# One decoder layer in split fp32 on one core: the embedding projection moves to the head of the program, and the last gate's K units are made and taken in another order

## The chip, the cores and the metric

The program runs on one core of a Trainium2 chip. The metric is the device time of one execution in microseconds (us); lower is better. The kernel before took 2470.43 us, the median of three runs (2469.58 to 2470.85).

## What is computed

One layer on `x` (512 tokens, width 2048), all in float32. Three additions to `x` follow each other, and the last one is the one that the change is about:

```python
x = x + jnp.concatenate([a_out, r_out], axis=-1) @ w_o[i]      # attention and retention heads

h2 = rms_norm(x, g_ffn[i])
x = x + (jax.nn.silu(h2 @ w_gate[i]) * (h2 @ w_up[i])) @ w_down[i]   # DFF = 5632

gate = jax.nn.sigmoid(rms_norm(x, g_ple[i]) @ w_ple_gate[i] + b_ple_gate[i])
x = x + (p[i] @ w_ple_proj[i]) * gate                           # p: 512 x 256, w_ple_proj: 256 x 2048
```

`p @ w_ple_proj`, here called **the projection**, depends on the inputs alone. The gate needs the finished `x` of the feed-forward part: its K dimension is the 2048 columns of that `x`.

## The kernel before, in words

**Precision.** Every float32 operand is split in two float32r parts, high and low (`split`, line 55): ScalarE (ACT) copies the high part, VectorE (DVE) subtracts it from the source for the low part. A product then takes three matmuls (`mm3`, line 78): high by high (line 79), high by low (line 80) and low by high (line 81). A weight unit is 128x1024 values, 512 KB: one load on the SP queue, one copy `wh` on ACT, one subtraction `wl` on DVE.

**The first part** (to line 446) makes attention and retention. `rows` (line 86) takes four PSUM banks from a pool that holds four (`acc_p`, line 51), multiplies, and hands each bank to an `evac`. At the head the 16 chunks of `x` come in, each multiplied by its gain and split (`gained`, line 132) and squared for the norm (`squares`, line 139), while the first product `qk_attn` runs over eight weight units. Here a list scheduler sets the order on each engine.

**The second part** multiplies with a scheme of seven products for each 2x2 block of quarters. `ORDER` (line 458) names them 1, 5, 6, 3, 7, 2, 4. Each product p has factors of the activation (`factors`, line 477: sums and differences of quarters, each split, 7 ACT copies, 7 DVE subtractions and 4 DVE sums for a pair of K chunks) and a weight that is the sum of quarters: for 5, 6, 7 and 4 DVE adds one loaded quarter into another in place (`Group.add`, line 533). Then come `extract` (line 546: `wh` on ACT, `wl` on DVE, three buffers) and `multiply` (line 556: 12 matmuls). A **step** is one product of one K unit. The loop at line 817 runs over the steps: at step i it adds for step i+3, extracts for step i+2 and multiplies step i. A finished product is evacuated two steps later (`evacuate`, line 604, `later(2, go)`). Quarters of the output are ready after products 3, 7, 2 and 4.

**Groups.** Eleven groups make gate and up (four units each), six make `w_down` (`down(kg, n)`, line 723: K in three parts, output in two halves n), two make the last gate (`gate(n)`, line 783: four units, output in two halves). The K units of the last gate are the columns of `x`: units 0 and 1 come from half n = 0 of the last down product and go through DRAM (`spill` into `s_h3`, then `reload`). Unit 3 (nh = 1) is complete after product 7 of `down(2, 1)`, unit 2 (nh = 0) after its product 4. Their factors (`to_factors`, line 667: eight PE transposes `tp<-ident`, then `factors`) are made 6 and 8 steps after product 7's evacuation for unit 3, and 1 and 3 steps after product 4's for unit 2. `split_order` (line 704) makes the first gate group run products 1, 5, 6 for units (0, 1), then for units (2, 3).

**The projection** stands between the last down group and the first gate group: four `Plain` steps (line 574), each with one unit of `w_pp`, 24 matmuls into `tp` banks, four copies by ACT (line 601, `pp<-tp`) and four stores to DRAM (`ppd`). `load_p` (line 768) loads `pT` and splits it when product 7 of the group before begins. The gate's `finish` (line 791) reads the projection back.

Of the kernel before, what the change touches and what calls it, by code (L numbers as in the profile page):

```python
# [10 lines left out]
F32 = mybir.dt.float32  # L11
F32R = mybir.dt.float32r
# [5 lines left out]
P = 128  # L18
T = 512
# [14 lines left out]
def layer_kernel(ctx, tc, xT, pT, g_mix, wqk, wv, wg, qk_norm, g_ret, w_o, g_ffn,  # L34
# [17 lines left out]
    at_p = mix_ctx.enter_context(tc.tile_pool(name="at_p", bufs=2, space=PSUM))  # L52

# [357 lines left out]

    qk, v = qk_attn(0, load_rest), v_of(0)
# [42 lines left out]
    dram = ctx.enter_context(tc.tile_pool(name="dram", bufs=1, space=bass.MemoryType.DRAM))  # L455
# [49 lines left out]
    def later(n, fn):  # L505
        due.setdefault(now[0] + n, []).append(fn)

    class Group:
        def __init__(self, src, units, tiles, evac, order=None, after=lambda p: None):
            self.src, self.units, self.tiles, self.evac, self.after = src, units, tiles, evac, after  # L510
            self.raw, self.bank, self.w, self.next, self.plains = {}, {}, {}, None, None
            self.left = {p: len(units) for p in ORDER}
            steps.extend((self, p, u) for p, u in
                         (order or [(p, u) for p in ORDER for u in range(len(units))]))
# [7 lines left out]
        def load_next(self, q, u):  # L522
            n = len(self.units)
            if q == "11" and self.plains:
                for v in [u] + (list(range(u + 1, NS)) if u == n - 1 else []):
                    self.plains[v].load()
            elif self.next is not None:
                m = len(self.next.units)
                for v in [u] + (list(range(n, m)) if u == n - 1 else []):
                    if v < m:  # L530
                        self.next.load(q, v)
# [42 lines left out]
    class Plain:  # L574

        def __init__(self, n):
            self.n, self.then = n, None
            steps.append((self, "p", 0))

        def load(self):  # L580
            self.raw = raw_ab.tile([P, 2, T], F32, name="raw", tag="l1")
            nc.sync.dma_start(self.raw, w_pp[self.n])

        def add(self, p, u):
            pass

        def extract(self, p, u):
            self.wh = wq.tile([P, 2, T], F32R, name="wh", tag="wh")
            self.wl = wq.tile([P, 2, T], F32R, name="wl", tag="wl")
            split(self.wh, self.wl, self.raw)  # L590
            self.then()

        def multiply(self, p, u):
            for b in range(NB):
                o = tp_p.tile([P, T], F32, name="tp", tag="tp")
                at = slice(b * P, (b + 1) * P)
                for c in range(2):
                    mm3(o, pTH[c][0][:, at], pTH[c][1][:, at], self.wh[:, c, :], self.wl[:, c, :],
                        c == 0, c == 1)
                t = ev_tile("g", 4, name="pp")  # L600
                nc.scalar.activation(t, o, AF.Copy)
                nc.sync.dma_start(ppd[b][:, self.n], t)

    def evacuate(finish, ahead=None):

        def evac(g, p):
# [30 lines left out]
            later(2, go)  # L637
# [6 lines left out]
    s_h3 = {p: dram.tile([P, 4, 2, 256], F32R, name=f"h3_{p}") for p in ORDER}  # L644
    xd = [[dram.tile([P, NS, T], F32, name=f"x{i}_{b}") for b in range(NB)] for i in range(4)]
    ppd = [dram.tile([P, NS, T], F32, name=f"pp_{b}") for b in range(NB)]
# [57 lines left out]
    split_order = [(p, u) for us in ((0, 1), (2, 3)) for p in "156" for u in us] + \  # L704
                  [(p, u) for p in "3724" for u in range(4)]

    def reload(tiles, where, n, wait={}):
        def go(p):
            tiles[p] = sp.tile([P, 8, 2, 256], F32R, name="s" + p, tag="s" + p)
            nc.sync.dma_start(tiles[p][:, :n].bitcast(F32), where[p].bitcast(F32))  # L710
        return lambda p: later(wait[p], lambda: go(p)) if p in wait else go(p)
# [11 lines left out]
    def down(kg, n):  # L723
# [7 lines left out]
        def finish(th, nh, b, part, t):  # L731
# [12 lines left out]
            for u in range(2):  # L744
                k = 4 * n + 2 * nh + u
                sink = spill(s_h3, k) if n == 0 else into(s_e, k)
                later((1 if n == 0 or nh == 0 else 6) + 2 * u, lambda u=u, sink=sink: to_factors(
                    lambda b: outs[b, nh], 2 * u, sink, lambda c: gp[:, 4 * s + c:4 * s + c + 1]))
# [16 lines left out]
    pTH = []  # L765
    bias_t = []

    def load_p():
        for k in range(2):
            raw = ev_tile("A")  # L770
            nc.sync.dma_start(raw, pT[k * P:(k + 1) * P, :])
            pTH.append([late_pools["ev2"].tile([P, T], F32R, name="pT", tag="o", bufs=4) for _ in range(2)])
            split(*pTH[k], raw)
# [6 lines left out]

    plains = [Plain(n) for n in range(NS)]
# [25 lines left out]
    groups[-3].plains = plains  # L807
    for n, pl in enumerate(plains):
        pl.then = lambda n=n: groups[-2].load("11", n)
# [4 lines left out]
    p_at = steps.index((groups[-3], "7", 0))  # L814
    b_at = steps.index((groups[-2], "3", 0))
    i = -3
    while i < len(steps) or due:
        now[0] = i
        if i == p_at:
            load_p()  # L820
        if i == b_at:
            load_bias()
        for n, act in ((3, "add"), (2, "extract"), (0, "multiply")):
            if 0 <= i + n < len(steps):
                g, p, u = steps[i + n]
                getattr(g, act)(p, u)
# [75 lines left out]
```

## Time and profile before

| | |
|---|---|
| median of three runs | 2470.43 us (2469.58 to 2470.85) |
| the profiled execution's own time | 2470.09 us |
| its span (first to last instruction) | 2468.3 us |
| TensorE (PE) busy | 2385.4 us, 97%, 11434 matmuls |
| DVE busy | 1836.6 us, 74% |
| ACT busy | 1091.5 us, 44% |
| moved by DMA | 390.27 MB |

How to read it: a matmul counts as busy for about 0.39 us though the next one begins 0.227 us after it, so PE's busy share says little on how full it is; its waits and the granted clock (PEclk, 1.00 is 2.4 GHz, 0.50 is 1.2 GHz) say more. The same holds on a smaller scale for DVE and ACT: two equal instructions in a row take less than twice the time of one.

### The profile page before, as it was taken

To read this page: it belongs to the slowest core of one execution; us is meant where nothing else is said; L and a number is where in the kernel's file an instruction comes from. 1 tells how busy PE (TensorE), PEld (TensorE's weight loads), DVE (VectorE), ACT (ScalarE), POOL (GpSimd) and SP (SyncE) were. 2 spreads that over 40 slices of the span, in tenths; PEclk is the share of its full clock that TensorE was granted. 3 is DMA by queue.
4 is the path that set the end of the run, shared out by engine and by line. 5 is a ranking of instruction groups with operands and counts; after the bars stand their busy time and mean duration, and the time that the engine had idled before them with its cause. 6 is when DMAs were issued, how large, how long until landed. Compare 5 with 4: busy or idle time off the path is not lost.

```text
span 2468.3 us, 30337 instructions
## 1 busy us (share of the span) xinstructions
PE 2385.4 (97%) x11434; PEld 1994.3 (81%) x11434; DVE 1836.6 (74%) x2469; ACT 1091.5 (44%) x1628; POOL 70.3 (3%) x63
## 2 busy tenths in 40 slices
PE   9999999999999986999999999999999999996998
PEld 7888888888888865888888888888878788884777
DVE  7585664546363688888988889888888778894897
ACT  5333333423232355545555455545544344463643
POOL 1122020000000000000000000000000000000000
PEclk9999999999999988999999999999999999998999
DMA  5222332333333333356434554445766956768263
GB/s 192 86 79 76 94 94 85 112 99 103 100 105 100 100 122 98 125 171 195 143 129 136 183 180 144 124 148 189 301 239 222 376 175 219 269 240 341 100 212 120
DMA packets 127988, 390.27 MB, mean 158 GB/s; under 512 B 14944, under 2 KB 15328, under 8 KB 124256
## 3 DMA queue, kind: packets, MB, share of 16 engines
q1 hardware_dynamic: 125136, 384.12, 46.5%
q10 hardware_dynamic: 2704, 4.20, 0.7%
q8 instruction: 90, 1.47, 0.3%
q14 instruction: 58, 0.48, 0.1%
HBM read 311.19 MB, written 72.88 MB: 156 GB/s over the span
## 4 chain that ended last, share of the span: by engine, by line
PE 85%; DVE 6%; DMA 5%; ACT 2%; issue 1%; ACTq 0%; SPq 0%; DVEq 0%
PE acc L80 10%; PE acc L81 10%; PE acc L79 10%; PE Y L80 7%; PE Y L79 7%; PE Y L81 7%; PE Z L80 5%; PE Z L81 5%; PE Z L79 5%; PE X L81 5%; PE X L80 5%; PE X L79 5%; DVE wl L59 2%; DVE raw L468 2%; PE at L80 1%
## 5 line engine op out<-in xcount | busy, mean ns | idle before, releaser
L58 ACT ACTIVATE wh<-raw 128x1024 fp32r<-128x1024 f32 (+1 forms) x667 | 705.9, 1059 | 946.3 <-PE Y L81 225.2
L59 DVE TENSOR_TENSOR wl<-raw,wh 128x1024 fp32r<-128x1024 f32 (+1 forms) x667 | 811.8, 1222 | 367.5 <-ACT wh L58 365.3
L468 DVE TENSOR_TENSOR raw<-raw 128x1024 f32<-128x1024 f32 x296 | 358.1, 1222 | 28.6 <-DMA raw<-in_w_gu 14.7
L80 PE MATMUL Y<-wl,s 128*128 128x512 f32 x888 | 349.6, 394 | 0.3 <-DVE wl L59 0.3
L81 PE MATMUL Y<-wh,s 128*128 128x512 f32 x888 | 346.9, 391 | 0.0
L79 PE MATMUL Y<-wh,s 128*128 128x512 f32 x888 | 311.6, 392 | 18.9 <-ACT wh L58 18.9
L80 PE MATMUL acc<-wl,actH 128*128 128x256 f32 (+1 forms) x768 | 244.1, 320 | 1.5 <-DVE wl L59 1.3
L81 PE MATMUL acc<-wh,actL 128*128 128x256 f32 (+1 forms) x768 | 243.6, 320 | 0.0
L79 PE MATMUL acc<-wh,actH 128*128 128x256 f32 (+1 forms) x768 | 239.7, 320 | 1.7 <-ACT wh L58 1.7
L80 PE MATMUL X<-wl,s 128*128 128x512 f32 x592 | 233.4, 395 | 5.9 <-DVE wl L59 5.7
L80 PE MATMUL Z<-wl,s 128*128 128x512 f32 x592 | 234.3, 396 | 3.5 <-DVE wl L59 3.4
L81 PE MATMUL X<-wh,s 128*128 128x512 f32 x592 | 232.1, 393 | 1.8 <-DVE s L59 1.8
L81 PE MATMUL Z<-wh,s 128*128 128x512 f32 x592 | 230.8, 391 | 0.0
L79 PE MATMUL X<-wh,s 128*128 128x512 f32 x592 | 210.1, 394 | 5.3 <-ACT wh L58 5.0
L79 PEld LDWEIGHTS Y<-wh,s 128*128 128x128 f32 x888 | 167.2, 189 | 55.2 <-ACT wh L58 20.4
L79 PE MATMUL Z<-wh,s 128*128 128x512 f32 x592 | 208.7, 393 | 0.9 <-ACT wh L58 0.9
L80 PEld LDWEIGHTS Y<-wl,s 128*128 128x128 f32 x888 | 167.4, 189 | 35.5 <-DVE wl L59 1.4
L81 PEld LDWEIGHTS Y<-wh,s 128*128 128x128 f32 x888 | 167.4, 189 | 34.0
L80 PEld LDWEIGHTS acc<-wl,actH 128*128 128x128 f32 x768 | 146.1, 190 | 12.6 <-DVE wl L59 2.5
L79 PEld LDWEIGHTS acc<-wh,actH 128*128 128x128 f32 x768 | 144.5, 190 | 12.6 <-ACT wh L58 2.8
L81 PEld LDWEIGHTS acc<-wh,actL 128*128 128x128 f32 x768 | 145.7, 190 | 9.9
L79 PE MATMUL acc<-actH,wh 128*128 128x512 f32 x384 | 149.9, 390 | 0.0
(184 smaller groups left out, 3370.2 us busy)
## 6 DMA issues: line engine op xcount, KB each, us to landing
raw<-in_w_gu SPq DMA_DIRECT2D x176, 512.0 KB, 4.3
raw<-in_w_dn SPq DMA_DIRECT2D x88, 512.0 KB, 5.8
a<-o SPq DMA_DIRECT2D x154, 256.0 KB, 2.9
raw<-in_wqk SPq DMA_DIRECT2D x63, 512.0 KB, 3.5
s<-a SPq DMA_DIRECT2D x14, 2048.0 KB, 11.1
raw<-in_wv SPq DMA_DIRECT2D x32, 512.0 KB, 3.5
raw<-in_w_o SPq DMA_DIRECT2D x32, 512.0 KB, 3.6
xin<-x SPq DMA_DIRECT2D x64, 256.0 KB, 5.5
```

The lines of the kernel that those rows point to most:

```text
L58: nc.scalar.activation(H, src, AF.Copy)
L59: nc.vector.tensor_tensor(L, src, H.bitcast(F32), op=ALU.subtract)
L79: nc.tensor.matmul(o, aH, bH, start=start, stop=False, skip_group_check=goes_on)
L80: nc.tensor.matmul(o, aH, bL, start=False, stop=False, skip_group_check=goes_on)
L81: nc.tensor.matmul(o, aL, bH, start=False, stop=stop, skip_group_check=goes_on)
L468: nc.vector.tensor_tensor(o, x, y, op=ALU.add)
```

## The change

Four things change.

- The projection's code leaves the step list (`Plain`, `load_p` and the `plains` hooks go). It stands now before the first `qk_attn`, written with `rows`: two chunks of `pT` loaded and split, then four times one unit of `w_pp`, 24 matmuls into the four `acc` banks, four ACT copies `pp<-acc` (line 423 of the changed kernel) and four stores.
- Unit 3's factors are made 1 and 2 steps after product 7's evacuation, inside the last group's products 2 and 4. Its factor for product 4, whose SBUF tile is still in use, goes through DRAM (`s_h3["4"]` grows from 4 to 6 chunks). Unit 2's follow 1 and 2 steps after product 4's evacuation.
- `split_order` becomes units (0, 1), then (3), then (2). It is shared by the first gate-up group.
- To allow runs of one unit, `extract` of step i+2 now comes before `add` of step i+3, and product 5 is evacuated one step after its end, not two.

```diff
+    ppd = [dram.tile([P, NS, T], F32, name=f"pp_{b}") for b in range(NB)]
+    pTH = []
+    for k in range(2):
+        raw = rp_tile("raw")
+        nc.sync.dma_start(raw, pT[k * P:(k + 1) * P, :])
+        pTH.append(qk_pair())
+        split(*pTH[k], raw)
+    for n in range(NS):
+        def pp_evac(b, acc, n=n):
+            t = rp_tile("pp")
+            nc.scalar.activation(t, acc, AF.Copy)
+            nc.sync.dma_start(ppd[b][:, n], t)
+        rows([w_pp[n]], lambda k: pTH[k], pp_evac)
+
     qk, v = qk_attn(0, load_rest), v_of(0)
...
-    class Plain:
...
-            later(2, go)
+            later(1 if p == "5" else 2, go)
...
-    s_h3 = {p: dram.tile([P, 4, 2, 256], F32R, name=f"h3_{p}") for p in ORDER}
+    s_h3 = {p: dram.tile([P, 6 if p == "4" else 4, 2, 256], F32R, name=f"h3_{p}") for p in ORDER}
...
-    split_order = [(p, u) for us in ((0, 1), (2, 3)) for p in "156" for u in us] + \
+    split_order = [(p, u) for us in ((0, 1), (3,), (2,)) for p in "156" for u in us] + \
                   [(p, u) for p in "3724" for u in range(4)]
...
-                sink = spill(s_h3, k) if n == 0 else into(s_e, k)
-                later((1 if n == 0 or nh == 0 else 6) + 2 * u, lambda u=u, sink=sink: to_factors(
+                sink = spill(s_h3, k)
+                if n == 1:
+                    direct = into(s_e, k)
+                    sink = (lambda p, a=spill(s_h3, k - 2 * nh), b=direct: a(p) if p == "4" else b(p)) if nh else direct
+                later((1 + 2 * u) if n == 0 else (1 + u), lambda u=u, sink=sink: to_factors(
...
-        for n, act in ((3, "add"), (2, "extract"), (0, "multiply")):
+        for n, act in ((2, "extract"), (3, "add"), (0, "multiply")):
```

What this makes of the order on the engines is shown at three places.

**ACT at the head.** `wh` and `qkH` are copies for a split, `actH` a chunk of `x` with its gain, `sq` and `total` its square, `pp` a bank of the projection. Before, the first rows with work are these:

```order
L141 ACTIVATE total<-x_98 128x512
L61 ACTIVATE actH<-x_98,gm 128x512
L58 ACTIVATE wh<-raw 128x512
L61 ACTIVATE actH<-x_99,gm 128x512
L143 ACTIVATE sq<-x_99 128x512
L58 ACTIVATE wh<-raw 128x512
L58 ACTIVATE wh<-raw 128x1024
```

Now the list begins with the splits of `pT` and of two units of `w_pp`. Then come all 16 chunks of `x`, with the squares of eleven of them, four copies for the projection's first unit and the splits of the third and fourth `w_pp` unit among them. Only after these 33 rows stand the copies that empty the second unit's banks, here the first `pp` row:

```order
L62 ACTIVATE actH<-x_114,gm 128x512
L144 ACTIVATE sq<-x_110 128x512
L62 ACTIVATE actH<-x_115,gm 128x512
L423 ACTIVATE pp<-acc 128x512 x2
L144 ACTIVATE sq<-x_111 128x512
L423 ACTIVATE pp<-acc 128x512 x2
L144 ACTIVATE sq<-x_112 128x512
L59 ACTIVATE wh<-raw 128x512 x2
L144 ACTIVATE sq<-x_113 128x512
L144 ACTIVATE sq<-x_114 128x512
L423 ACTIVATE pp<-acc 128x512
L144 ACTIVATE sq<-x_115 128x512
```

The last `pp` row of this list belongs to the third unit; three more of it, with the norm's `sqs` among them, follow, and the fourth unit's four come after the next `wh`.

**PE where the last down group ends.** `Y_18616` and `Y_18837` are banks of its product 4, `tp<-wh,pT` is the projection, `X` a bank of the gate's product 1. Before:

```order
L80 MATMUL Y_18616<-wl,s_17545 128x512
L81 MATMUL Y_18616<-wh,s_17545 128x512
L79 MATMUL tp<-wh,pT 128x512
L80 MATMUL tp<-wl,pT 128x512
L79 MATMUL tp<-wh,pT 128x512
```

Now, with transposes `tp<-ident` of unit 3 in product 4 itself:

```order
L653 MATMUL tp<-ident,v 128x128 x2
L653 MATMUL tp<-ident,e_18533 128x128
L653 MATMUL tp<-ident,e_18534 128x128
L81 MATMUL Y_18836<-wl,s_17741 128x512
...
L81 MATMUL Y_18837<-wl,s_17741 128x512
L82 MATMUL Y_18837<-wh,s_17741 128x512
L81 MATMUL X_18942<-wl,s_18529 128x512
```

The gate's matmuls follow the last down matmul directly.

**DVE in the gate's single-unit steps.** `raw<-raw` adds weight quarters, `wl` is the subtraction of a weight, `s<-` and `t<-` are parts of `factors`. The last steps before product 3 read now:

```order
L482 TENSOR_TENSOR raw<-raw 128x1024
L479 TENSOR_TENSOR t_19072<-A,t_19071 128x256
L60 TENSOR_TENSOR wl<-raw,wh 128x1024
L60 TENSOR_TENSOR s_18531<-t_19071,s_18531 128x256
L479 TENSOR_TENSOR t_19074<-A,t_19072 128x256
L479 TENSOR_TENSOR t_19073<-A,t_19072 128x256
L60 TENSOR_TENSOR s_18569<-t_19072,s_18569 128x256
L482 TENSOR_TENSOR raw<-raw 128x1024
L60 TENSOR_TENSOR s_18636<-t_19074,s_18636 128x256
L60 TENSOR_TENSOR s_18702<-t_19073,s_18702 128x256
L60 TENSOR_TENSOR wl<-raw,wh 128x1024 x3
```

One weight is added to, split, added to again and split again, and the factors of unit 2 stand between. Between the head and the last down group the orders differ in a few rows near the first gate-up group's start (its unit 3 now before its unit 2); DVE's next 835 instructions stand as before.

## Rows read from the trace of the kernel before

**Rows 1.** The first section of the page: busy time of each engine, its share of the span, and instructions.
```profile
PE 2385.4 (97%) x11434; PEld 1994.3 (81%) x11434; DVE 1836.6 (74%) x2469; ACT 1091.5 (44%) x1628; POOL 70.3 (3%) x63
```

**Rows 2.** Busy time of each engine in stretches from the last down group into the first gate group; columns: stretch, its length, busy time of PE, its weight loads, DVE, ACT and POOL with their instructions, granted clock, DMA share, GB/s.
```profile
2205.00:2222.00 17.00, 17.00 (x79) 14.08 (x78) 16.67 (x26) 10.36 (x16) 0.00 (x0) 1.00 0.91 308
2222.00:2241.00 19.00, 18.93 (x84) 15.35 (x82) 16.62 (x26) 8.89 (x13) 0.00 (x0) 1.00 0.98 352
2241.00:2284.00 43.00, 19.06 (x58) 13.44 (x58) 8.57 (x12) 15.18 (x29) 0.00 (x0) 0.72 0.86 337
2284.00:2324.00 40.00, 36.55 (x167) 29.29 (x167) 36.08 (x62) 27.89 (x54) 1.01 (x1) 0.99 0.30 106
...
2254.00:2265.00 11.00, 4.01 (x9) 2.73 (x10) 0.69 (x1) 1.71 (x3) 0.00 (x0) 0.53 1.02 415
```

**Rows 3.** What PE waited for between 2165 and 2300 us: total, times, longest.
```profile
PE tp L79 <- ACT pT L58: 16.9, 2, 10.0
PE tp L79 <- ACT pp L601: 6.5, 2, 6.3
```

**Rows 4.** PE's matmuls in order of time: start, duration, line, operation, tiles, and in brackets the wait before it. The last down matmuls, the projection's first and some later ones, the gate's first matmul, and the first two of its product 3.
```profile
2240.32 0.39 PE L80 MATMUL Y<-wl,s 128*128 128x512 f32 x1
2240.54 0.39 PE L81 MATMUL Y<-wh,s 128*128 128x512 f32 x1
2247.83 0.80 PE L79 MATMUL tp<-wh,pT 128*128 128x512 f32 x1 [6.90 <-ACT pT L58]
2248.85 0.63 PE L79 MATMUL tp<-wh,pT 128*128 128x512 f32 x1
2249.28 0.63 PE L80 MATMUL tp<-wl,pT 128*128 128x512 f32 x1
...
2260.73 0.80 PE L79 MATMUL tp<-wh,pT 128*128 128x512 f32 x1 [9.97 <-ACT pT L58]
...
2283.45 0.73 PE L79 MATMUL X<-wh,s 128*128 128x512 f32 x2 [0.29 <-ACT wh L58]
...
2336.10 0.61 PE L79 MATMUL Z<-wh,s 128*128 128x512 f32 x2
```

**Rows 5.** The SP queue: when the two loads of `pT` were issued.
```profile
2227.67 0.33 SPq L771 DMA_DIRECT2D A<-in_pT  x1
...
2248.74 0.39 SPq L771 DMA_DIRECT2D A<-in_pT  x1
```

**Rows 6.** ACT in order of time: the split of the second `pT` chunk, and one of the projection's copies.
```profile
2260.05 0.63 ACT L58 ACTIVATE pT<-A 128x512 fp32r<-128x512 f32 x1 [6.41 <-DMA A<-in_pT]
...
2276.74 0.60 ACT L601 ACTIVATE pp<-tp 128x512 f32<-128x512 f32 x1 [2.44 <-PE tp L81]
```

**Rows 7.** DVE in order of time in the last down group: instructions of each size, pairs in one row (x2), and the instruction from which the sum below counts (the second evacuation of product 6).
```profile
2204.42 2.36 DVE L59 TENSOR_TENSOR wl<-raw,wh 128x1024 fp32r<-128x1024 f32 x2
...
2209.76 0.69 DVE L465 TENSOR_TENSOR v<-Y,e 128x512 f32<-128x512 f32 x1
2210.36 1.22 DVE L59 TENSOR_TENSOR wl<-raw,wh 128x1024 fp32r<-128x1024 f32 x1
2211.50 0.76 DVE L465 TENSOR_TENSOR t<-A,t 128x256 f32<-128x256 f32 x2
...
2226.02 1.28 DVE L465 TENSOR_TENSOR e<-Y,e 128x512 f32<-128x512 f32 x2
```

**Rows 8.** ACT in order of time at the head, and the first 30 us as in rows 2.
```profile
9.18 0.71 ACT L61 ACTIVATE actH<-x,gm 128x512 fp32r<-128x512 f32 x1
9.79 0.62 ACT L143 ACTIVATE sq<-x 128x512 f32<-128x512 f32 x1
10.31 0.71 ACT L61 ACTIVATE actH<-x,gm 128x512 fp32r<-128x512 f32 x1
...
17.21 1.04 ACT L58 ACTIVATE wh<-raw 128x1024 fp32r<-128x1024 f32 x1
18.15 0.71 ACT L61 ACTIVATE actH<-x,gm 128x512 fp32r<-128x512 f32 x1
...
0.00:30.00 30.00, 25.98 (x103) 18.55 (x104) 23.85 (x37) 24.34 (x39) 0.20 (x4) 1.00 0.81 274
```

**Rows 9.** PE in order of time at the head: its first real matmul, and its two waits.
```profile
5.35 1.20 PE L79 MATMUL acc<-wh,actH 128*128 128x512 f32 x4
...
18.30 1.19 PE L79 MATMUL acc<-wh,actH 128*128 128x512 f32 x4 [1.65 <-ACT wh L58]
20.64 0.50 PE L80 MATMUL acc<-wl,actH 128*128 128x512 f32 x1 [1.15 <-DVE wl L59]
```

**Rows 10.** The chain that ended last, at its beginning: start, duration, what. The load is the fifth; 1536 KB had been asked for with it.
```profile
2.59 5.60 DMA raw<-in_wqk
8.21 1.06 ACT wh L58
```

**Rows 11.** PE where the first gate-up group begins, in order of time, and the stretch around it as in rows 2.
```profile
947.53 1.22 PE L79 MATMUL Y<-wh,s 128*128 128x512 f32 x2 [16.34 <-ACT wh L58]
...
952.44 0.63 PE L80 MATMUL Y<-wl,s 128*128 128x512 f32 x1
952.86 0.63 PE L81 MATMUL Y<-wh,s 128*128 128x512 f32 x1
...
930.00:958.00 28.00, 8.94 (x27) 6.35 (x26) 25.06 (x52) 18.36 (x40) 0.00 (x0) 0.57 0.33 113
```

More of the change, by code (lines that the diff above doesn't have):

```diff
@@ L52, in layer_kernel @@
     at_p = mix_ctx.enter_context(tc.tile_pool(name="at_p", bufs=2, space=PSUM))
+    dram = ctx.enter_context(tc.tile_pool(name="dram", bufs=1, space=bass.MemoryType.DRAM))
     def split(H, L, src, scale=None):
@@ L454, in layer_kernel @@
     chain = ctx.enter_context(pool("chain", 1, space=PSUM))
-    dram = ctx.enter_context(tc.tile_pool(name="dram", bufs=1, space=bass.MemoryType.DRAM))
     late_pools = {}
@@ L510, in __init__ @@
             self.src, self.units, self.tiles, self.evac, self.after = src, units, tiles, evac, after
-            self.raw, self.bank, self.w, self.next, self.plains = {}, {}, {}, None, None
+            self.raw, self.bank, self.w, self.next = {}, {}, {}, None
             self.left = {p: len(units) for p in ORDER}
@@ L523, in load_next @@
             n = len(self.units)
[L524 to L527, printed above, removed]
+            if self.next is not None:
                 m = len(self.next.units)
@@ L572, in multiply @@
                 self.evac(self, p)
-    class Plain:
[L576 to L602, printed above, removed]
     def evacuate(finish, ahead=None):
@@ L643, in layer_kernel @@
     s_a = [{p: dram.tile([P, n, 2, 256], F32R, name=f"a{i}_{p}") for p in ORDER} for i, n in enumerate(KG)]
-    s_h3 = {p: dram.tile([P, 4, 2, 256], F32R, name=f"h3_{p}") for p in ORDER}
+    s_h3 = {p: dram.tile([P, 6 if p == "4" else 4, 2, 256], F32R, name=f"h3_{p}") for p in ORDER}
     xd = [[dram.tile([P, NS, T], F32, name=f"x{i}_{b}") for b in range(NB)] for i in range(4)]
-    ppd = [dram.tile([P, NS, T], F32, name=f"pp_{b}") for b in range(NB)]
     for i in range(NC // 2):
@@ L709, in go @@
             tiles[p] = sp.tile([P, 8, 2, 256], F32R, name="s" + p, tag="s" + p)
-            nc.sync.dma_start(tiles[p][:, :n].bitcast(F32), where[p].bitcast(F32))
+            nc.sync.dma_start(tiles[p][:, :n].bitcast(F32), where[p][:, :n].bitcast(F32))
+            if where is s_h3 and p == "4":
+                nc.sync.dma_start(tiles[p][:, 6:].bitcast(F32), where[p][:, 4:].bitcast(F32))
         return lambda p: later(wait[p], lambda: go(p)) if p in wait else go(p)
@@ L762, in layer_kernel @@
                                 s_d[kg], down(kg, n), None, after))
-    pTH = []
     bias_t = []
[L768 to L773, printed above, removed]
     def load_bias():
@@ L779, in load_bias @@
             bias_t.append(t)
-    plains = [Plain(n) for n in range(NS)]
     def gate(n):
@@ L806, in layer_kernel @@
         a.next = b
-    groups[-3].plains = plains
-    for n, pl in enumerate(plains):
-        pl.then = lambda n=n: groups[-2].load("11", n)
     for q in ("11", "12", "22"):
@@ L813, in layer_kernel @@
             groups[0].load(q, u)
-    p_at = steps.index((groups[-3], "7", 0))
     b_at = steps.index((groups[-2], "3", 0))
@@ L818, in layer_kernel @@
         now[0] = i
-        if i == p_at:
-            load_p()
         if i == b_at:
             load_bias()
-        for n, act in ((3, "add"), (2, "extract"), (0, "multiply")):
+        for n, act in ((2, "extract"), (3, "add"), (0, "multiply")):
             if 0 <= i + n < len(steps):
```

## The prediction

> **What bounds the kernel now.** I read the page's busy times first: PE is the busiest engine by far [rows 1], so a change pays where PE stands still. Next the waits of PE by stretch, and there one place stands out: between the last down group and the gate, PE waits 16.9 us for the splits of `pT` and 6.5 us for the projection's copies [rows 3]. The table by stretch shows what that place costs: from 2241 to 2284 PE issues 58 matmuls at a mean granted clock of 0.72, while the stretches before it run at 1.00 with PE full [rows 2]. At full speed a 512-column matmul follows the one before it after 0.227 us (2240.32, 2240.54 and on); inside the projection they stand 0.43 apart (2248.85, 2249.28), which is the lower level of 1.2 GHz, after a pause of 6.90 us [rows 4]. 50 matmuls at 0.227 and 8 short transposes of some 0.11 are 12.2 us of work in 43: **about 31 us are lost there.** The cause stands on the queue: the second `pT` load is issued 21 us after the first [rows 5], ACT waits 6.41 us for it [rows 6], and the DMA engines are then full (share 1.02 at 415 GB/s) [rows 2]. So the projection, meant to fill the time in which the gate's factors are made, waits itself.
>
> **What goes.** I measure the late stage from a point that both orders share, DVE's second evacuation of product 6 in the last down group, at 2209.76 [rows 7], to the first matmul of the gate's product 3, at 2336.10 [rows 4]: **126.3 us** before.
>
> **What stands there now.** The projection's 96 matmuls (21.8 us at 0.227) are gone from it, with their loads, splits, copies and stores. The rest is not PE's time alone, since all four `to_factors` calls of units 3 and 2 now fall into the steps of products 2 and 4 and the gate's first twelve. Counted in the new order, DVE has 117 instructions between the two points: 36 of 1024 elements, 62 of 256, 17 of 512 and two tiny ones. Two of 1024 in a row take 2.36 where one takes 1.22, so each takes 1.14; in the same way two of 256 take 0.76 and two of 512 1.28, one 0.69, which makes 0.34 and 0.60 [rows 7]. That is 41.0 + 21.1 + 10.2 + 0.3 = **72.6 us**. PE's own work in it, some 280 matmuls and 32 transposes, is 67 us, so DVE becomes the bound of this stage. After DVE's last subtraction PE still has the 12 matmuls of that step, 2.7 us. To this I add what DVE waits for. In the single-unit steps of products 5 and 6 a weight is added to, copied by ACT (1.04 us [rows 8]) and subtracted, one after the other, four times in all: 4.2 us if nothing fills them. And at its fullest DVE was busy for 16.67 of 17.00 us [rows 2], which is 1.4 us of small gaps here. The bounds are 75.3 (no wait at all) and 84 (all waits, and the last 12 matmuls at the lower clock, 2.4 more). I take 72.6 + 2.7 + 4.2 + 1.4, or **81**, since the order shows little between an addition and its subtraction. The late stage goes from 126.3 to 81, that is **-45.3 us**.
>
> **What is added at the head.** With no limit but PE the projection would take its 21.8 us there and a later start. The order on ACT is the limit. The four first loads are 1536 KB together; before, the load that completed as many bytes landed at 8.19 [rows 10], so ACT's second `wh` runs from 8.2 to 9.2. From there ACT has, in its order, 16 gained chunks at 0.61, 11 squares at 0.52, two `wh` at 0.94 [rows 8] and four copies at 0.50 (one lasts 0.60 [rows 6], a square 0.62 and 0.52 apart) before it may empty the second unit's banks: 19.4 us, to 28.6. The third unit needs these four banks, since the pool has four. The four copies and one square take to 31.1, then a square, two half splits and two squares to 33.7; the third unit's copies are done at 34.2, 35.2, 35.7 and, behind the norm's split, 36.8. The fourth unit's 24 matmuls run after these, to about 40.5. So `qk_attn` begins at **40.5 where it began at 5.35** [rows 9], 35.2 later. It then finds all of `x` split, and the two early waits of 1.65 and 1.15 [rows 9] should not return: **+32.4 us**, of which 21.8 is the projection and 10.6 is PE standing. Lower bound: ACT doesn't hold PE up, 21.8 less the two waits, +19. Upper: the third and fourth unit's 48 matmuls run at the lower clock and none of it is hidden, 0.2 each, +42.
>
> **What costs nothing.** The `w_pp` loads and stores share SP's queue with `x`; the first `wqk` load stands behind the stores of the first unit, whose last copy runs near 20 us, and must land by 40, so 20 us of the projection cover it. If the head were quick, the load would be late by some 5 us. Product 5's earlier evacuation needs two copies and one `wh` on ACT within one step, 1.0 + 0.95 of 2.72 us: nothing, or a microsecond in each of two groups. The swap of `extract` and `add` leaves DVE's order in the long middle as it was. In the first gate-up group unit 3 now comes before unit 2; the wait of 16.34 us there [rows 11] is before product 6 of the first units and stays. Its slow matmuls after it, 0.42 apart (952.44, 952.86), can come a few more or fewer: 0, within 3 us either way. Unit 3's factors for product 4 go out in two stores of 256 KB and come back with a reload that is read some twenty steps later.
>
> **The sum.** 2470.1 (the profiled execution's own time, 0.3 below the median of the runs) + 32.4 - 45.3 + 0 = **2457 us**.
>
> **Rivals.**
>
> *The head is lighter.* If the evacuations reach ACT earlier than I reckon, since ACT's instructions are partly shorter than I took them, the head costs +24 to +28 and the time is 2449 to 2453. For it: PE alone needs only 21.8. Against: the copies stand behind 33 rows on an engine that was busy for 24.34 of the first 30 us without the projection [rows 8].
>
> *The late stage stays long.* Either transfers bind again, or unit 2 is late all the same. The four rates from 2205 to 2324 times their lengths are 31 MB [rows 2], of which 7 go (`pT`, `w_pp` and 16 stores of 256 KB); 24 MB at 352 GB/s are 68 us and fit into 81, at 258, the mean over that time, they are 93. Or unit 2's chain of evacuation, transposes, copies and splits overruns the nine steps, 24 us at 12 matmuls each, that cover it. The stage then takes 90 to 93, and the time is 2466 to 2469: no change that can be told.
>
> *The clock at the head, slower.* PE now pauses between the second and third unit, from about 19 to 29 us. In the trace a pause of 9.97 us is followed by matmuls at the lower level, and after one of 16.34 us they were still 0.42 apart 5 us later [rows 4, 11]. The Trainium skill ("TensorE: Matmul & The Clock Gate", section "HAM oscillation — how this bites in real kernels") says that a matmul stream broken by waits falls back to half rate and starts cold after each of them, and by that rule moving the projection into a place with pauses gives part of the gain back. The trace agrees as far as the late stage goes (0.53 in 2254 to 2265 [rows 2]); no run here shows the head. By the rows the price is 0.2 us a matmul. In my forecast the 48 of the third and fourth unit wait for ACT anyway, so a slow start costs 0 to 5 us. The change would be slower if the lower level held through the fourth unit and the first three `qk_attn` units, 24 + 72 matmuls at 0.2, or 19 us: 2476. It decides from about 13 us, some 65 matmuls. Against it: PE is dense from 34 us on, and from 2284, PE busy again, the clock was at 0.99 [rows 2].
>
> *The change doesn't do what it says:* unit 3's factors could still wait for the tiles of the running group. The order shows their transposes inside product 4, so I give this little, within the second rival.
>
> **Chances.** Forecast, within 6 us of 2457: 0.60. Lighter head: 0.16. Late stage long: 0.17. Slow clock or other trouble at the head: 0.07. A measurement of this kernel can tell about 0.2%, 5 us, from no change. Faster by more: the first two and a little of the third, 0.79; the same: 0.15; slower: 0.06. The range runs from the lighter head to the late stage at its longest, **2447 to 2468**; what lies outside is the slow clock and a stage that gains nothing.
>
> **What would show each step.** Right: `qk_attn` begins at 38 to 43 us, with a PE wait of 7 to 11 us for an ACT `wh` or a bank near 20 to 29 us; no `pT` wait after 2200; DVE over 95% busy in the 70 us before the gate's product 3, which begins 77 to 84 us after the shared point. Wrong: a head under 30 us (evacuations earlier), PE idle with DVE idle too in the late stage (transfers, or unit 2's chain), or PEclk under 0.9 well past 45 us.

## The result and the profile after

The changed kernel took **2455.11 us** (median of four runs, 2454.82 to 2460.03) beside 2470.01 for the kernel before (four runs, 2468.43 to 2470.85): a ratio of 0.9945, interval 0.9928 to 0.9962. Five more runs later gave 2458.18 (2455.01 to 2462.65) and a ratio of 0.9944, interval 0.993 to 0.9957. The profiled execution took 2455.12 us with a span of 2453.3, against 2470.09 and 2468.3. The forecast of 2457.0 and its range hold.

The 15.0 us between the two profiled executions divide as follows. Up to the late stage each figure is how much more, or less, a matmul's start has shifted at the stretch's end than at its beginning, matmuls being counted from `qk_attn`'s first, without the two of the norm (`tp<-sqs`), which changed their place; the late stage has its own measure, below.

| stretch | forecast | measured |
|---|---|---|
| head, to 64 us of before | +32.4 | +32.9 |
| rest of the first part | 0 | -1.3 |
| start of the feed-forward part | 0, within 3 | -3.4 |
| from there to the late stage | 0 | +1.8 |
| late stage | -45.3 | -46.1 |
| after it, to the last matmul | 0 | +1.1 |

**The head.** PE in order of time, as in [rows 9]: the first matmul of the projection, the first of its third unit and of its fourth, and the first of `qk_attn`, and then ACT, as in [rows 8].

```profile
8.27 1.77 PE L80 MATMUL acc<-wh,qkH 128*128 128x512 f32 x4 [2.75 <-ACT wh L59]
...
29.34 0.79 PE L80 MATMUL acc<-wh,qkH 128*128 128x512 f32 x1 [8.20 <-ACT pp L423]
...
36.39 0.39 PE L80 MATMUL acc<-wh,qkH 128*128 128x512 f32 x1
...
42.33 0.39 PE L80 MATMUL acc<-wh,actH 128*128 128x512 f32 x1
```

```profile
8.40 1.06 ACT L59 ACTIVATE wh<-raw 128x1024 fp32r<-128x1024 f32 x1 [0.19 <-DMA raw<-in_w_pp]
...
28.09 0.71 ACT L62 ACTIVATE actH<-x,gm 128x512 fp32r<-128x512 f32 x1
28.70 1.06 ACT L423 ACTIVATE pp<-acc 128x512 f32<-128x512 f32 x2
```

ACT reaches the copies that empty the second unit's banks at 28.70, where the count of 33 rows gave 28.6, and PE waits 8.20 us for them. `qk_attn` begins at 42.33, 1.8 later than forecast. The third unit took 7.05 us (29.34 to 36.39), where 24 matmuls at 0.227 are 5.4: from 29.93 to 32.49 they stand 0.43 apart, the lower clock level. And the norm's two `tp<-sqs` now stand ahead of `qk_attn`, 0.46 us. From 42 to 60 us the granted clock is 1.00.

**The late stage.** First PE's waits between 2240 and 2320 (total, times, longest), as in [rows 3]; then stretches as in [rows 2].

```profile
PE Y L80 <- ACT wh L59: 2.5, 2, 1.9
PE Z L81 <- DVE wl L60: 2.5, 2, 2.1
PE Y L81 <- DVE wl L60: 0.9, 1, 0.9
```

```profile
2239.70:2320.00 80.30, 73.66 (x315) 57.46 (x314) 75.43 (x121) 49.99 (x94) 1.11 (x1) 0.96 0.80 301
...
2290.00:2310.00 20.00, 16.54 (x72) 11.99 (x71) 19.99 (x41) 15.32 (x36) 1.11 (x1) 0.98 0.63 236
2310.00:2320.00 10.00, 7.89 (x22) 5.63 (x21) 6.27 (x8) 4.33 (x7) 0.00 (x0) 0.70 0.14 43
```

The waits of 16.9 and 6.5 us are gone. DVE is busy for 75.4 of 80.3 us, and for all of 2290 to 2310, when the DMA engines are no longer full. The first two matmuls of product 3 now stand among product 6's, so I end the stage at the matmul that has as many behind it as product 3's first had before: it starts at 2319.97, and the shared point is 2239.73 (both below). That is **80.2 us** against 126.3, where 77 to 84 was to show the forecast right; to product 3's first matmul by the letter, at 2315.98, it is 76.3.

The last ten microseconds differ from my picture: DVE is busy for 6.27 of 10.00. DVE in order of time, then ACT, then PE:

```profile
2239.73 0.68 DVE L479 TENSOR_TENSOR v<-Y,e 128x512 f32<-128x512 f32 x1
...
2310.21 1.21 DVE L482 TENSOR_TENSOR raw<-raw 128x1024 f32<-128x1024 f32 x1
2311.35 0.75 DVE L60 TENSOR_TENSOR s<-t,s 128x256 fp32r<-128x256 f32 x2
2315.01 3.50 DVE L60 TENSOR_TENSOR wl<-raw,wh 128x1024 fp32r<-128x1024 f32 x3 [2.92 <-ACT wh L59]
```

```profile
2312.95 1.09 ACT L603 ACTIVATE e<-Z 128x512 f32<-128x512 f32 x2 [2.54 <-PE Z L82]
2313.92 2.95 ACT L59 ACTIVATE wh<-raw 128x1024 fp32r<-128x1024 f32 x3
```

```profile
2309.00 0.62 PE L81 MATMUL Z<-wl,s 128*128 128x512 f32 x1 [2.08 <-DVE wl L60]
...
2312.40 0.74 PE L82 MATMUL Z<-wh,s 128*128 128x512 f32 x2
2315.03 0.73 PE L80 MATMUL Y<-wh,s 128*128 128x512 f32 x2 [1.89 <-ACT wh L59]
...
2319.97 0.39 PE L81 MATMUL Y<-wl,s 128*128 128x512 f32 x1
```

The last weight's sum was ready at 2311.4, but on ACT the two evacuations of product 5, which now come one step after its end, stand ahead of three `wh`. They wait 2.54 us for PE, DVE waits 2.92 for the first `wh`, and PE 1.89. PE was late for its part: it had waited 2.08 us for a `wl` of DVE, and the ten matmuls from there on stand 0.43 apart, at the lower clock level (a mean clock of 0.72 from 2309 to 2315). So in these last microseconds the three engines wait for each other, and DVE's work does not set the time.

**The start of the feed-forward part.** The same 300 matmuls in the changed kernel, and in a second profiled execution of it; columns as in [rows 11]. Before they took 103.9 us, at a mean clock of 0.80.

```profile
920.20:1020.70 100.50, 70.80 (x301) 55.21 (x301) 84.28 (x141) 61.77 (x118) 1.01 (x1) 0.83 0.40 136
```

```profile
921.00:1025.10 104.10, 73.46 (x302) 57.43 (x301) 85.17 (x141) 61.89 (x118) 1.01 (x1) 0.80 0.39 134
```

The same program took 3.6 us more the second time, at a mean clock of 0.80 for 0.83. The gain of 3.4 us here can therefore not be put down to the change: the pause of 16.3 us stayed, and how much of the slow stretch around it falls at the lower level differs from one execution to the next.

**Two small terms.** The +1.8 ahead of the late stage arises in one place, at 1811 to 1830 us of before: there PE waits 1.9 us for a `wh` and 1.3 for a DVE `t`, at a mean clock of 0.87, where it had waited 1.1, 0.7 and 0.5 at 0.95. Every version below in which the projection has moved has the wait of 1.9 us; why is open. Of the +1.1 after the late stage 0.6 is a wait for a `wl` at 2326.62.

### The profile page after: what moved, and what is told of

The parts are those of the page before. It is cut to its first block, busy times and chain, and to the rows that moved or that the text cites. A ratio compares the mean times of both kernels' runs of the same rounds, so it can differ in the third digit from the quotient of the medians.

```text
span 2453.3 us, 30345 instructions
## 1 busy us (share of the span) xinstructions
PE 2382.6 (97%) x11434; PEld 1992.3 (81%) x11434; DVE 1836.2 (75%) x2469; ACT 1087.9 (44%) x1628; POOL 70.0 (3%) x63
## 4 chain that ended last, share of the span: by engine, by line
PE 85%; DVE 7%; DMA 3%; ACT 2%; issue 2%; SPq 0%; DVEq 0%; ACTq 0%
PE acc L80 11%; PE acc L81 11%; PE acc L82 11%; PE Y L81 7%; PE Y L82 7%; PE Y L80 7%; PE Z L81 5%; PE Z L82 5%; PE Z L80 5%; PE X L81 5%; PE X L80 5%; PE X L82 5%; DVE wl L60 2%; DVE raw L482 2%; PE at L81 1%
## 5 line engine op out<-in xcount | busy, mean ns | idle before, releaser
L59 ACT ACTIVATE wh<-raw 128x1024 fp32r<-128x1024 f32 x667 | 705.4, 1059 | 966.3 <-PE Y L82 229.6
L60 DVE TENSOR_TENSOR wl<-raw,wh 128x1024 fp32r<-128x1024 f32 x667 | 809.5, 1219 | 366.6 <-ACT wh L59 364.0
```

Of the source, the lines that this page charges most:

```text
L59: nc.scalar.activation(H, src, AF.Copy)
L60: nc.vector.tensor_tensor(L, src, H.bitcast(F32), op=ALU.subtract)
```

## The experiments

All are measured against the kernel before. Experiments 1 to 4, 5 to 8 and 9 to 12 ran on three chips, each beside runs of the kernel before on the same chip, so between them the ratios compare better than the times. The late stage is measured as above, in each one's profiled execution; the rows give its length, the busy times of PE, its weight loads, DVE, ACT and POOL, the granted clock, DMA share and GB/s. Five profiled executions have the change's code for this stage unaltered: the change in two executions, and experiments 3, 4 and 12. In them it took 80.2, 80.6, 78.6, 81.2 and 79.5 us, which is the spread to read the other lengths by.

### 1. The projection's move alone

```diff
 # the kernel before, with the projection's code at the head as in the change:
...
+        rows([w_pp[n]], lambda k: pTH[k], pp_evac)
...
-    plains = [Plain(n) for n in range(NS)]
...
```

> The kernel before with only the projection moved to the head; unit 3's factors stay at 6 and 8 steps, units 2 and 3 run as a pair, adds stand before extracts, product 5 is evacuated two steps after its end. Theory (the projection and its transfers were what made the late stage long, and DVE's work is the bound once they are gone): the late stage, from the shared point to the gate's product 3, takes 82 to 90 us, the head costs 32 to 33 as in the change, and the time is 2456 to 2465. Rival (the early factors and the new order of units are what shortens the stage): it stays over 100 us, and the time is 2474 or more.

Measured: 2459.0 us (2458.32 to 2462.28), ratio 0.9956, interval 0.9943 to 0.997. The late stage took 82.7 us:

```profile
2243.75:2326.48 82.73, 72.44 (x314) 57.97 (x313) 75.65 (x121) 51.01 (x94) 14.30 (x1) 0.94 0.76 280
```

Of the 46.1 us that the change gains there, the move alone gives 43.6; the other 2.5 are hardly more than the spread. PE now waits 5.9 us once, for ACT's `s`, a factor of the second pair of units.

### 2. Units 3 and 2 as a pair

```diff
-    split_order = [(p, u) for us in ((0, 1), (3,), (2,)) for p in "156" for u in us] + \
+    split_order = [(p, u) for us in ((0, 1), (3, 2)) for p in "156" for u in us] + \
```

> The change, but with units 3 and 2 as a pair in products 1, 5 and 6 (unit 3 first) and not one after the other; the first gate-up group takes the same order. Theory (the four waits of add, copy and subtract in single-unit steps, 4.2 us of my sum, go): the time is 2449 to 2453, the late stage 75 to 78. Rival (the run of unit 3 alone is what gives unit 2's factors their time): PE waits for unit 2's factors in product 1, the stage is 82 to 88 and the time 2457 to 2463.

Measured: 2452.7 us (2451.51 to 2454.3), ratio 0.9931, interval 0.9919 to 0.9944.

```profile
2243.10:2318.05 74.95, 69.62 (x314) 55.11 (x312) 73.81 (x119) 49.17 (x93) 5.74 (x1) 1.00 0.85 317
```

What DVE waited for in it:

```profile
DVE wl L60 <- ACT wh L59: 0.5, 2, 0.3
```

DVE's idle time in the stage falls from 4.9 us to 1.1 and the stage by 5.3; DVE's work is the same within 2 us. Product 5 is evacuated as early here as in the change. Running unit 3 alone, then unit 2, makes the late stage longer.

### 3. The projection before the feed-forward part

```diff
     rms_of(total, two_rm(), total, D, rstd2)
+    # pT, split and the four rows([w_pp[n]], ...) stand here, not at the head
     mix_ctx.close()
```

> The change, but the projection's code stands at the end of the first part, before the feed-forward begins, where PE paused 16.3 us for the factors. Theory (the projection costs only what PE has to add where it is not waiting; the head's 10.6 us of standing belong to the head): qk_attn begins at 5 to 6 us, the pause is filled for the most part, and the time is 2433 to 2441. Rival (ACT and DVE, for which that pause waits, get the copies and splits of the projection in their order, and the pause comes after it all the same): 21.8 us and 16.3 us stand one behind the other, and the time is 2444 to 2452.

Measured: 2440.53 us (2439.2 to 2442.41), ratio 0.9882, interval 0.9868 to 0.9895: the theory's time, but not by the pause that I named. PE's waits around that place, in the change from 880 to 1000 us, then here from 880 to 970:

```profile
PE Y L80 <- ACT wh L59: 16.3, 1, 16.3
PE tp L155 <- ACT sqs L59: 6.0, 1, 6.0
```

```profile
PE Y L80 <- ACT wh L59: 16.0, 1, 16.0
```

The long pause stays at 16.0, as the rival had it; what the projection fills is the wait of 6.0 us for the norm, which came before it. The matmul behind the long pause starts at 947.53 before [rows 11], at 976.52 in the change and at 963.33 here, so 29.0 and 15.8 us later. Of the 15.8 us, 4.2 were there before the projection: in this execution PE's mean clock was 0.86 from 20 to 43 us, where the kernel before had 1.00 from 20 to 40. The projection's 21.8 us of work thus cost 11.6 here; the wait for the norm accounts for 6.0 of the rest, and the remaining 4.2 are not traced.

### 4. Eight banks at the head

```diff
-        accs = [bank() for _ in range(NB)]
+        accs = [bank() for _ in range(NB)] if n % 2 == 0 else \
+            [at_p.tile(...) for _ in range(2)] + [tp_p.tile(...) for _ in range(2)]
```

> The change, but the projection's second and fourth unit take the two banks each of the pools at and tp, so that no unit waits for the one just before it to be emptied. Theory (the third unit stands because the four banks are emptied behind ACT's chunks of x): the wait of 8.2 us shrinks to 1 to 4, qk_attn begins at 34 to 37 us, and the time is 2447 to 2451. Rival (the splits of the third and fourth w_pp unit, which stand behind the same chunks on ACT, end last): PE then waits for wh instead, qk_attn begins at 40 to 42, and the time is 2454 to 2456.

Measured: 2449.78 us (2447.73 to 2450.01), ratio 0.9917, interval 0.9903 to 0.9931. PE from 6 to 46 us:

```profile
22.73 1.20 PE L80 MATMUL acc<-wh,qkH 128*128 128x512 f32 x4 [2.50 <-ACT wh L59]
...
35.69 0.39 PE L80 MATMUL acc<-wh,actH 128*128 128x512 f32 x1
```

The wait of 8.2 us for a bank is gone, one of 2.50 for the unit's `wh` takes its place, and `qk_attn` begins 6.6 us earlier. So the four banks, emptied in ACT's order, held PE up.

### 5. More work on DVE

```diff
             split(H, L, made[p])
+            if late:
+                nc.vector.tensor_tensor(L, made[p], H.bitcast(F32), op=ALU.subtract)
```

`late` is true for the factors of units 2 and 3 alone, here and in experiments 6 and 11.

> The change, but the low part of every factor of units 2 and 3 (four calls, 28 instructions of 256 elements) is subtracted twice on DVE; the values stay what they are. At 0.34 each that is 9.5 us of DVE work more in the late stage. Theory (DVE's work sets the length of that stage): the 6.5 us in which DVE waits there for wh and for weight loads can take up a part, so the stage grows from 80.2 to 85 to 90, and the time is 2459 to 2465. Rival (transfers, or PE and ACT by turns, set it, and DVE is only busy beside them): the stage stays within 2 us, and the time is 2454 to 2457.

Measured: 2460.14 us (2459.19 to 2460.83), ratio 0.996, interval 0.9948 to 0.9973.

```profile
2242.60:2325.70 83.10, 74.17 (x314) 57.82 (x313) 82.50 (x146) 51.05 (x94) 21.36 (x1) 0.94 0.76 286
```

The time lies in the theory's range, but the stage met neither length: it grew by 2.9 us, not by 5 or more. DVE was busy 7.1 us longer, and its idle time fell from 4.9 to 0.6 us, the waits for `wh` in it from 4.0 to 0.5. So the added work first filled DVE's waits, and only what did not fit there made the stage longer.

### 6. The factors' low parts on POOL

```diff
-            split(H, L, made[p])
+            if late:
+                nc.scalar.activation(H, made[p], AF.Copy)
+                nc.gpsimd.tensor_tensor(L, made[p], H.bitcast(F32), op=ALU.subtract)
+            else:
+                split(H, L, made[p])
```

> The change, but those 28 subtractions run on POOL, which stands in this stage and takes about 1.05 us for a 128x256 operation of the first part. Theory (DVE sets the stage): DVE has 9.5 us less, the stage falls to 71 to 77, and the time is 2445 to 2451. Rival (POOL, three times as slow, makes unit 2's factors late, or its work slows DVE's): PE waits for POOL's s, the stage takes 79 to 85, and the time is 2454 to 2460.

Measured: 2457.96 us (2455.45 to 2461.97), ratio 0.9952, interval 0.9939 to 0.9964; the stage took 81.2. The rival holds, in both of its parts: PE waits 2.5 us for POOL's `s`, and DVE's instructions are slower. DVE's groups from 2240 to 2320 (count, busy, mean ns), in the change and then here:

```profile
L60 DVE TENSOR_TENSOR wl<-raw,wh 128x1024 fp32r<-128x1024 f32 x24 | 28.9, 1216 | 4.0 <-ACT wh L59 4.0
L482 DVE TENSOR_TENSOR raw<-raw 128x1024 f32<-128x1024 f32 x14 | 17.0, 1214 | 0.0
L479 DVE TENSOR_TENSOR t<-A,t 128x256 f32<-128x256 f32 x17 | 6.6, 415 | 0.0
...
L479 DVE TENSOR_TENSOR e<-Y,e 128x512 f32<-128x512 f32 x4 | 2.6, 681 | 0.0
```

```profile
L60 DVE TENSOR_TENSOR wl<-raw,wh 128x1024 fp32r<-128x1024 f32 x23 | 30.4, 1333 | 2.7 <-ACT wh L59 2.7
L482 DVE TENSOR_TENSOR raw<-raw 128x1024 f32<-128x1024 f32 x14 | 20.0, 1430 | 0.1
L479 DVE TENSOR_TENSOR t<-A,t 128x256 f32<-128x256 f32 x17 | 10.9, 667 | 0.1
...
L479 DVE TENSOR_TENSOR e<-Y,e 128x512 f32<-128x512 f32 x4 | 2.6, 681 | 0.0
```

In these three groups alone DVE's instructions take 10 us longer in sum (117 ns by 23, 216 by 14, 252 by 17), as much as the 9.5 us that were taken off it. The means mix two durations, which the last section tells apart.

### 7. An earlier `pT` in the old place

```diff
-            raw = ev_tile("A")
-            nc.sync.dma_start(raw, pT[k * P:(k + 1) * P, :])
...
+            for h in range(2):
+                at = slice(256 * h, 256 * h + 256)
+                raw = ev_tile("t", 4, 256, "praw")
+                nc.sync.dma_start(raw, pT[k * P:(k + 1) * P, at])
+                split(pTH[k][0][:, at], pTH[k][1][:, at], raw)
```

> The kernel before, with the projection in its old place, but both chunks of pT are loaded through the four t tiles, which are free then, in halves, so that the second chunk need not wait for an A tile. Theory (what the projection costs there are its loads and stores, its few banks and its splits behind other work, not one late load): PE waits about as long, now for the projection's banks and weights, and the time is 2465 to 2472. Rival (the late pT load is the cause, and the projection could have stayed): the waits for pT, 16.9 us, go, and the time is 2453 to 2461.

Measured: 2471.16 us (2469.2 to 2474.26, eleven runs), ratio 1.0006, interval 0.9998 to 1.0015. The stage took 125.9. PE's waits from 2225 to 2345:

```profile
PE tp L79 <- ACT pT L58: 12.5, 2, 7.1
PE tp L79 <- ACT pp L601: 8.0, 2, 7.7
```

The `pT` wait shrinks by 4.4 and others grow. The second chunk's loads are issued 5.8 us earlier than before [rows 5]. The SP queue, the time from issue to landing of the four `pT` loads (least, median, most), and ACT's split of that chunk:

```profile
2242.92 1.06 SPq L774 DMA_DIRECT2D praw<-in_pT  x2
```

```profile
DMA to landing us min/median/max: 6.6/7.4/7.9
```

```profile
2257.55 0.72 ACT L58 ACTIVATE pT<-praw 128x256 fp32r<-128x256 f32 x2 [9.35 <-DMA h<-o]
```

The chunk had landed by 2251.4, and yet its split began at 2257.55, when a store `h<-o` had landed. The tiles for the split `pT` are taken from the four tiles of `o`, through which factors go to DRAM, and must wait until these are stored. In the kernel before, the last two such stores landed at 2254.67 and 2259.06 and the late load at 2259.97: taken in the same order, the split's high part could have come some 5 us earlier without that load, its low part 0.9. So one late load was not the cause. Whether the projection could have stayed there with tiles of its own, no run shows.

### 8. Experiments 2 and 3 together

The edit is the two diffs above in one kernel.

> The third and the second experiment together: the projection before the feed-forward part, and units 3 and 2 as a pair. Theory (the two act at different places and add up: 14.6 us less there, 2.4 here): the late stage takes 74 to 77, and the time is 2434 to 2440. Rival (the gate's loads are now what DVE waits for in the late stage, so that the pair gives nothing more): 2440 to 2443.

Measured: **2434.6 us** (2432.21 to 2434.88), ratio 0.9855, interval 0.984 to 0.987, the fastest version; its stage took 75.6. The two gains add up within the noise: by the ratios 0.0063 and 0.0014 below the change's 0.9945 make 0.9868.

### 9 and 10. The change again, and the factors made as late as before

The ninth is the change without an edit; the tenth:

```diff
...
-                    sink = (lambda p, a=spill(s_h3, k - 2 * nh), b=direct: a(p) if p == "4" else b(p)) if nh else direct
+                    sink = direct
-                later((1 + 2 * u) if n == 0 else (1 + u), lambda u=u, sink=sink: to_factors(
+                later((1 if n == 0 or nh == 0 else 6) + 2 * u, lambda u=u, sink=sink: to_factors(
```

> The change itself once more, as the measure for the other three of this call, which differ from it by a few us. Expected by every theory: 2453 to 2458 us.

> The change, but unit 3's factors are made 6 and 8 steps after product 7's evacuation, and unit 2's 1 and 3 steps after product 4's, as before the change, so that none goes through DRAM; unit 3 still runs alone before unit 2. Theory (DVE has the same instructions in the late stage either way, and the factors come in time): the stage takes 77 to 83, and the time is 2451 to 2457. Rival (the early factors are a real part of the gain, since unit 3's would now be late for its own steps): PE waits for unit 3's s, the stage takes 85 or more, and the time is 2459 to 2466.

Measured: the change 2458.18 us as told above, a little over what was expected, its stage 80.6; with late factors 2452.45 (2450.47 to 2456.31), ratio 0.9924, interval 0.9912 to 0.9937. The late factors' stage, what DVE waited for in it, and ACT at the place where it stood for PE in the change:

```profile
2242.35:2318.10 75.75, 70.89 (x315) 56.24 (x314) 74.22 (x120) 50.47 (x94) 21.39 (x1) 0.98 0.82 300
```

```profile
DVE wl L60 <- ACT wh L59: 1.3, 2, 0.7
```

```profile
2313.32 2.01 ACT L59 ACTIVATE wh<-raw 128x1024 fp32r<-128x1024 f32 x2 [1.05 <-DVE raw L482]
...
2315.53 0.58 ACT L603 ACTIVATE e<-Z 128x512 f32<-128x512 f32 x1
```

The rival falls, and the stage is shorter than the theory had it. Made late, unit 3's factors stand between the gate's additions and subtractions and give DVE something to do there, and on ACT the `wh` comes before `e<-Z`. The early factors, a part of the change, cost 4.5 to 4.8 us of the stage against the change's two executions, 2.8 to 5.4 against all five.

### 11. Less work on DVE

```diff
-            split(H, L, made[p])
+            if late:
+                nc.scalar.activation(H, made[p], AF.Copy)
+                nc.scalar.activation(L, made[p], AF.Copy, scale=0.0)
+            else:
+                split(H, L, made[p])
```

> The change, but ACT writes the low parts of the factors of units 2 and 3 (as copies times zero, so these low parts are left out of the result), and DVE has those 28 subtractions less, 9.5 us at 0.34, with nothing on POOL. Theory (DVE sets the late stage, and POOL's work beside it took the gain away in the run before): the stage falls to 71 to 77, and the time is 2446 to 2452. Rival (DVE's work is not what sets it; the chain from weight load by addition, copy and subtraction to PE is): the stage stays at 79 to 82, and the time is 2453 to 2457.

Measured: 2447.63 us (2446.21 to 2449.99), ratio 0.9904, interval 0.989 to 0.9917.

```profile
2239.00:2312.40 73.40, 69.67 (x315) 55.38 (x314) 65.01 (x92) 56.49 (x121) 1.11 (x1) 1.00 0.88 328
```

DVE's work falls by 10.4 us and the stage by 6.9, with the clock at 1.00. PE waits 3.8 us in all, and its own work was reckoned at 67, so it is then the nearer limit. So DVE's work does set most of the stage in the change, and the next limit lies some 7 us below it.

### 12. Eight banks, emptied by DVE

```diff
-            nc.scalar.activation(t, acc, AF.Copy)
+            nc.vector.tensor_scalar(t, acc, 1.0, None, op0=ALU.mult)
```

> The fourth experiment, with the projection's banks emptied by DVE instead of ACT. Theory (what stands between PE and the projection's end at the head is the emptying of banks in ACT's order): PE's wait for a bank, 8.2 us in the change, goes whole, qk_attn begins at 29 to 34 us, and the time is 2443 to 2448. Rival (DVE has the low parts of the chunks of x in its order just as ACT has the high parts, or the w_pp splits bind): qk_attn begins at 35 to 37 as in the fourth experiment, and the time is 2448 to 2452.

Measured: 2448.79 us (2447.49 to 2450.34), ratio 0.9908, interval 0.9894 to 0.9921, the same as experiment 4 within the noise. PE at the head:

```profile
22.97 0.79 PE L81 MATMUL acc<-wl,qkH 128*128 128x512 f32 x1 [2.43 <-DVE wl L60]
...
35.78 0.39 PE L80 MATMUL acc<-wh,actH 128*128 128x512 f32 x1
```

```profile
19.00:30.00 11.00, 8.22 (x23) 6.21 (x24) 11.00 (x18) 6.59 (x11) 0.00 (x0) 0.69 0.94 286
```

The rival holds. The third unit starts at 19.35, 3.4 us earlier than in experiment 4, then waits 2.43 us for DVE's `wl`, and the stretch runs at a mean clock of 0.69 where experiment 4 had 0.84.

## Why the prediction was right, and where it was off

- **The head (+32.4, measured +32.9).** ACT's 33 rows took what was reckoned, and experiment 4 shows that they act through the four banks. Of the slow start that I put at 0 to 5 us some 1.6 came in the third unit, and the lower level did not last. That the sum is met within 0.5 us is in part luck: `qk_attn` began 1.8 later than reckoned, and after it 4.1 us came back where I had reckoned 2.8 for the two waits. The lighter head did not come about; in experiment 12 a wait for `wl` and the lower clock level took back what an earlier start had won.
- **What made the late stage long.** That it was the projection with all that belongs to it is shown by experiment 1. My reading that the cause stood on the queue, in the second `pT` load, is not borne out: in experiment 7 that load was in time, and the split waited for a tile that was still being stored. How much the transfers, the tiles and the banks each cost there is not separated.
- **The late stage (-45.3, measured -46.1).** That DVE's work then sets most of it is shown by experiments 2, 5 and 11 together. The terms came out less exact than their sum: 72.6 us of work in 117 instructions and 1.4 of gaps were 75.4 busy in 121, and of the 2.7 us behind DVE's last subtraction only 0.8 were idle time of DVE. These two errors nearly cancel, which is luck. The 4.2 us for waits were the right size, with 4.0 measured (2.92 in one place), but not by their reason. I put them on four additions with nothing between; three quarters came from ACT, where product 5's earlier evacuation stood ahead of `wh`. I had priced that evacuation at nothing or a microsecond: **this is the term that was mis-sized.** This is read from one place of the trace; no run changed that evacuation alone. It is as early in experiments 2 and 10, where DVE waits 0.5 and 1.3 us for `wh`, so it costs this much only together with units taken one by one and early factors. DVE was busy for 93% of the last 70 us (65.1), where I had said over 95, and for some two microseconds PE and DVE stood at once, which I had named as a sign of being wrong, though for other reasons.
- **What the parts are worth.** I took the change as one. The move of the projection alone gives nearly all; early factors together with units 3 and 2 one by one make the late stage longer than either late factors or the pair (75.7 and 75.0 us, experiments 10 and 2). In the whole time that difference is near the noise.
- **The feed-forward start** was put at 0 within 3; it was -3.4 in one execution and +0.2 in another of the same kernel.
- **The +1.8 and the +1.1** were not in the sum.

What stays open: the pause of 16 us at the feed-forward start, which no run here filled.

## What to carry to other kernels

Work that depends on the inputs alone can go where PE waits for something else. What it cost at the head was decided by the engine that empties its banks, so count that engine's rows ahead of the emptying. Where it waits for an input, ask not only when the load lands but also when the tile that it is copied into comes free. When an engine becomes the bound of a stage, as DVE did here, its waits are the place for work that can be moved; making that work earlier takes the filling away. In an engine's fixed order look at what waits behind each evacuation, not only at how long it lasts.

## What the runs showed of the hardware

POOL's subtractions of 128x256 took 1.26 to 1.34 us in the mean in experiment 6 and slowed DVE's instructions beside them. In single instructions it is one duration or the other: DVE's additions and subtractions with both inputs in SBUF took 0.41 us at 256 elements and 1.21 at 1024 on their own, and 0.94 to 0.96 and 1.64 to 1.76 when a POOL subtraction that had begun before them had half a microsecond or more to run: about half a microsecond longer at either size. Where DVE's had begun first (2268.71, 2278.51), it kept its 1.2 us and POOL's took 1.8 instead of 0.9. Three of DVE's instructions:

```profile
2275.30 0.68 DVE L479 TENSOR_TENSOR e<-Y,e 128x512 f32<-128x512 f32 x1
...
2292.26 0.96 DVE L479 TENSOR_TENSOR t<-A,t 128x256 f32<-128x256 f32 x1
2293.15 1.76 DVE L482 TENSOR_TENSOR raw<-raw 128x1024 f32<-128x1024 f32 x1
```

The Trainium skill ("SBUF — State Buffer", section "Who interferes with whom") says that a DVE instruction with two SBUF inputs contends with a GpSimd instruction that reads SBUF, and that one with at most one SBUF input, outside the modes that use both of DVE's ports, does not. The trace agrees with the first half. For the second it has one instruction, `e<-Y,e` at 2275.30, with one input in a PSUM bank: beside a POOL subtraction that began at 2275.05 it took 0.68 us, as such instructions do on their own.

One kernel took 2455.12 and 2460.71 us in its two profiled executions, 5.6 us apart, of which 3.6 lay in the 300 matmuls around the 16 us pause. On one chip five of its runs went from 2455.01 to 2462.65.
